# Addresses modulo 256 of the streamed tiles and of the low weight slices in a one-core decoder layer

## The chip, the cores and the metric

The kernel runs on one core of a Trainium2 chip. The metric is the device time of one execution in microseconds, here the median of three runs. Engines are named as in the profile: PE is TensorE's matmul, PEld TensorE's weight load, DVE VectorE, ACT ScalarE, POOL GpSimd, SP SyncE (which issues most DMAs).

## The reference

One layer of a hybrid decoder, on 256 prompt positions and 8 x 4 sample positions, which the kernel holds as 288 columns:

```python
x = x + 0.5 * swiglu(rms_norm(x, g1), w_gate1, w_up1, w_down1)      # D_MODEL 2048, D_FF 5632
z = rms_norm(x, gm) @ w_in                                           # u | q | k | v
y_ssm  = s5_mixer(u, ...)       # complex diagonal SSM, then GLU
y_attn = window_attention(q, k, v, ...)   # window 128, 16 query heads, 4 kv heads
x = x + concat(rms_norm(y_ssm), rms_norm(y_attn)) @ w_out
x = x + 0.5 * swiglu(rms_norm(x, g2), w_gate2, w_up2, w_down2)
```

All of it is in float32. The large matrix products (gate, up, down, w_in, w_out) make up nearly all of TensorE's work.

## The kernel before

**Three products for one.** Activations and weights are each split into a high part (rounded to the matmul's type fp32r) and a low part (the rest). One product of a 128 x 128 weight block with 128 x 288 activations is three matmuls, in `mm3` (L266 to L272): high weights by high activations (L270), high weights by low activations (L271), low weights by high activations (L272). Every matmul comes with a weight load of its own, so the high slice is loaded twice. While matmul j streams its 288 columns, TensorE loads the weights of matmul j+1; "streamed tile" is the moving operand, one of `xh[k]`, `xl[k]`, `hh`, `hl` (128 partitions x 288 values of 4 bytes, 1152 bytes in a partition), and "slice" is a weight block of 128 x 128 values (512 bytes in a partition).

So the loads go like this: while L270 streams the high tile of k, the high slice a is loaded again (for L271); while L271 streams the low tile of k, the low slice a is loaded (for L272); while L272 streams the high tile of k, the high slice a+1 is loaded (for the next L270).

**The stream of weights.** `Weights` walks a list of 680 pieces (up to 8 slices, 512 KB each; the down projection's are of 6 and 5 slices). `load` (L76) issues a DMA into a `raw` tile on SP's queue, `split` (L84) makes `wh` on ACT (L88) and `wl` on DVE (L89), and `next` (L102) hands one piece to the matmuls. Program order keeps the splits two pieces ahead of the matmuls and the loads five pieces ahead. A `raw` tile may be loaded again when its split is done; there are five. `wh` and `wl` have three buffers each.

**The stages.** `ffn(0)` runs first, to about 870 us; then `mix` (w_in, SSM and attention work, w_out), to about 1185 us; then `ffn(1)`. In `ffn`, gate and up (`gu`, streaming xh and xl, 16 values of k) fill a ring of h tiles, `hh` and `hl` of 13 buffers each, and after every 11 of them `down(c)` streams those 11 tiles for each of 16 output tiles: 33 matmuls to an output tile. w_out streams 8 tiles of pools with 8 buffers each.

**Addresses.** A partition's byte address of each tile follows from the order and sizes of the allocations. 1152 is 4 x 256 + 128, so tiles that follow one another alternate between two classes modulo 256 that are 128 apart. As the program is laid out:
- `xh[0]` and `xl[0]` both start at 128 modulo 256, since 16 tiles are a whole number of 256. So the order of streaming in gate, up and w_in is 128, 128, 128, then 0, 0, 0, and so on by k: three streamed tiles of one class, then three of the other. w_out's tiles (8 buffers each) go in the same way.
- `hh` and `hl` of a ring of 13 are in opposite classes, since 13 tiles are an odd number of 128. So the down projections stream a high, a low and a high tile of alternate classes, and the next k goes on alternating, except where the ring wraps and where one output tile ends and the next begins (tile 11 and tile 1 are of one class). The two classes are 64 and 192 in ffn(0), 32 and 160 in ffn(1), and all four in w_out.
- `wh` and `wl` buffers are 4096 bytes and start at 160 modulo 256, and slices are 512 bytes apart: every slice that is loaded starts at 160.

So in ffn(1)'s down projections a load is either in the very class of the tile that is streamed beside it (160 and 160) or in the opposite one (160 and 32), in turn. In the other stages the two are 32, 96, 160 or 224 apart.

## Time and profile before

| | |
|---|---|
| median of three runs | 2029.94 us (2029.13 to 2031.17) |
| the profiled execution | 2029.67 us |
| its span, first to last instruction | 2027.9 us |
| PE busy | 2006.7 us (99%) |
| matmuls of L270, L271 and L272 | 14400 (9408 stream xh or xl, 4992 stream hh or hl) |
| mean granted TensorE clock | 0.998 |

Busy times of PE count overlapping matmuls once. Since a matmul is recorded from its first column to its last result, about 295 ns, and the next one starts about 132 ns later, the pace of TensorE is read from the starts: in a stretch without other work, the time between two starts divided by the number of matmuls between them. The count is in the views too: a window's count is the steps in it and the two or three matmuls that reach into it from ahead or start at its end.

### The profile page before, as it was taken

To read this page: it belongs to the slowest core of one execution; us is meant where nothing else is said; L and a number is where in the kernel's file an instruction comes from. 1 tells how busy PE (TensorE), PEld (TensorE's weight loads), DVE (VectorE), ACT (ScalarE), POOL (GpSimd) and SP (SyncE) were. 2 spreads that over 40 slices of the span, in tenths; PEclk is the share of its full clock that TensorE was granted. 3 is DMA by queue.
4 is the path that set the end of the run, shared out by engine and by line. 5 is a ranking of instruction groups with operands and counts; after the bars stand their busy time and mean duration, and the time that the engine had idled before them with its cause. 6 is when DMAs were issued, how large, how long until landed. Compare 5 with 4: busy or idle time off the path is not lost. (4 is left out here: it accounts for less than half of the span.)

```text
span 2027.9 us, 37632 instructions
## 1 busy us (share of the span) xinstructions
PE 2006.7 (99%) x15248; PEld 1994.0 (98%) x15248; DVE 1211.4 (60%) x1873; ACT 850.6 (42%) x1334; POOL 296.1 (15%) x451
## 2 busy tenths in 40 slices
PE   8999999999999999999999999999999999999999
PEld 8999999999999999999989999999999999999999
DVE  5577666666656645676687874445445544454444
ACT  5433443444344434533466443333333333333332
POOL 3100011001110000212268630000000000000000
PEclk9999999999999999999999999999999999999999
DMA  6655656564556554678733445555555655565554
GB/s 225 201 163 151 211 162 197 170 209 166 196 169 196 180 198 140 215 231 269 237 118 131 152 161 166 166 149 181 167 166 151 186 162 166 149 180 170 167 158 149
DMA packets 122622, 359.04 MB, mean 177 GB/s; under 512 B 22448, under 2 KB 30256, under 8 KB 121264
## 3 DMA queue, kind: packets, MB, share of 16 engines
q1 hardware_dynamic: 114672, 340.81, 53.3%
q10 hardware_dynamic: 7776, 15.83, 2.3%
q8 instruction: 119, 1.95, 0.4%
q14 instruction: 55, 0.45, 0.1%
HBM read 338.40 MB, written 20.22 MB: 177 GB/s over the span
## 5 line engine op out<-in xcount | busy, mean ns | idle before, releaser
L89 DVE TENSOR_TENSOR wl<-raw,wh 128x1024 fp32r<-128x1024 f32 (+2 forms) x680 | 759.6, 1118 | 539.4 <-ACT wh L88 536.4
L270 PE MATMUL main<-xh,wh 128*128 128x288 f32 x3136 | 935.7, 298 | 6.2 <-ACT xh L178 6.2
L272 PE MATMUL main<-xh,wl 128*128 128x288 f32 x3136 | 932.7, 297 | 0.3 <-DVE wl L89 0.3
L271 PE MATMUL main<-xl,wh 128*128 128x288 f32 x3136 | 918.2, 293 | 1.3 <-DVE xl L179 1.3
L88 ACT CAST wh<-raw 128x1024 fp32r<-128x1024 f32 (+2 forms) x680 | 642.9, 946 | 625.2 <-PE main L271 414.8
L271 PEld LDWEIGHTS main<-xl,wh 128*128 128x128 f32 x3136 | 600.9, 192 | 2.4 <-DVE xl L179 2.1
L270 PEld LDWEIGHTS main<-xh,wh 128*128 128x128 f32 x3136 | 592.2, 189 | 7.3 <-ACT xh L178 6.2
L272 PEld LDWEIGHTS main<-xh,wl 128*128 128x128 f32 x3136 | 590.4, 188 | 0.6 <-DVE wl L89 0.6
L270 PE MATMUL main<-hh,wh 128*128 128x288 f32 x1664 | 494.4, 297 | 0.0
L271 PE MATMUL main<-hl,wh 128*128 128x288 f32 x1664 | 492.2, 296 | 0.3 <-DVE hl L667 0.3
L272 PE MATMUL main<-hh,wl 128*128 128x288 f32 x1664 | 491.4, 295 | 0.0
L271 PEld LDWEIGHTS main<-hl,wh 128*128 128x128 f32 x1664 | 313.6, 188 | 0.7 <-DVE hl L667 0.6
L270 PEld LDWEIGHTS main<-hh,wh 128*128 128x128 f32 x1664 | 313.6, 188 | 0.4
L272 PEld LDWEIGHTS main<-hh,wl 128*128 128x128 f32 x1664 | 313.7, 189 | 0.0
L296 POOL TENSOR_TENSOR s<-s,R 128x288 f32<-128x288 f32 x88 | 71.5, 812 | 1252.0 <-ACT s L295 1252.0
L295 ACT ACTIVATE s<-t 128x288 f32<-128x288 f32 x88 | 39.1, 445 | 237.9 <-DVE t L294 237.9
L303 ACT CAST hh<-h 128x288 fp32r<-128x288 f32 x88 | 38.1, 433 | 240.0 <-DVE h L302 240.0
L323 DVE SCALAR_TENSOR_TENSOR x<-main,x 128x288 f32<-128x288 f32 x128 | 58.3, 456 | 50.0 <-PE main L272 48.2
L302 DVE TENSOR_TENSOR h<-main,s 128x288 f32<-128x288 f32 x88 | 40.2, 457 | 77.4 <-PE main L272 76.9
L294 DVE TENSOR_TENSOR t<-main,R 128x288 f32<-128x288 f32 x88 | 40.2, 457 | 64.1 <-PE main L272 63.4
L304 DVE TENSOR_TENSOR hl<-h,hh 128x288 fp32r<-128x288 f32 x88 | 40.3, 458 | 43.9 <-ACT hh L303 43.9
L188 POOL TENSOR_TENSOR acc<-acc,sq 128x288 f32<-128x288 f32 x45 | 48.8, 1085 | 56.7 <-ACT sq L184 55.3
(263 smaller groups left out, 879.3 us busy)
## 6 DMA issues: line engine op xcount, KB each, us to landing
raw<-in_w_gu SPq DMA_DIRECT2D x352, 512.0 KB, 3.6
raw<-in_w_dn SPq DMA_DIRECT2D x128, 384.0 KB, 3.1
raw<-in_w_dn SPq DMA_DIRECT2D x128, 320.0 KB, 3.0
raw<-in_w_in SPq DMA_DIRECT2D x40, 512.0 KB, 4.2
raw<-in_w_out SPq DMA_DIRECT2D x32, 512.0 KB, 3.4
mats<-stage ACTq DMA_DIRECT2D x8, 1536.0 KB, 7.0
mb<-mats SPq DMA_DIRECT2D x8, 768.0 KB, 6.7
ma<-mats SPq DMA_DIRECT2D x8, 512.0 KB, 4.3
```

The costliest lines, as they stand in the source:

```text
L88: self.nc.scalar.copy(wh[:, :n], t[:, :n])
L89: self.nc.vector.tensor_tensor(wl[:, :n], t[:, :n], wh[:, :n].bitcast(F32), op=ALU.subtract)
L188: eng.tensor_tensor(acc, acc, sq, op=ALU.add)
L270: pe.matmul(ps, wh[:, s], rh[k], start=first and a == 0, stop=False)
L271: pe.matmul(ps, wh[:, s], rl[k], start=False, stop=False)
L272: pe.matmul(ps, wl[:, s], rh[k], start=False, stop=last and a == n - 1)
L294: dve.tensor_tensor(t1, pg[:, :N], R, op=ALU.mult)
L295: act.activation(s1, t1, AF.Silu)
L296: pool_e.tensor_tensor(s2, s1, R, op=ALU.mult)
L302: dve.tensor_tensor(h, pu[:, :N], s2, op=ALU.mult)
L304: dve.tensor_tensor(hl, h, hh.bitcast(F32), op=ALU.subtract)
L323: dve.scalar_tensor_tensor(x[d], ps[:, :N], 0.5, x[d], op0=ALU.mult, op1=ALU.add)
```

## The change

- A tile of 128 bytes (`gap_x`) is allocated between `xh` and `xl`, and one of 128 bytes between `hh` and `hl` of the rings and of the w_out pools (`gap_r`, `gap_y`). The rings have 14 buffers in place of 13. So the high and the low tile of a k are in opposite classes, and the streamed tiles alternate in every stage, still except from one output tile of a down projection to the next (11 tiles).
- `wl`'s slices are 640 bytes apart (`WLS` is 160 values), so that they alternate between two classes as well: slice a starts at 128 x a modulo 256. `wl` tiles are 5376 bytes in place of 4096. For chunks of the down projection whose first tile falls on an odd place of the ring, the slices start 128 bytes later (`shifted`). DVE's subtraction writes through a three-dimensional pattern, 8 x 128 with a step of 160.
- `gap_w`, `gap_p` and `gap_l` bring the pools behind them to the class that this needs: with `gap_x` and `gap_w`, the constants end at a multiple of 256, and `wh` and `wl` start at 0 modulo 256.
- `raw` has four buffers in place of five, which makes room.

No instruction is added or taken away, and none is moved in any queue. `wh`'s slices stay 512 bytes apart, so all of them start at 0 modulo 256, while the tiles streamed beside them go 128, 0, 128 for one k (high, low, high) and 0, 128, 0 for the next. Counted over six matmuls (two values of k), the loads beside the streamed tiles are: opposite class, same, opposite; same, same, same.

```diff
+WLS = P + 32
+RING = 14
...
-        t = self.pool.tile([P, HALF], F32, name="raw", bufs=5)
+        t = self.pool.tile([P, HALF], F32, name="raw", bufs=4)
...
-        wl = self.pool.tile([P, HALF], F32R, name="wl", bufs=3)
+        wl = self.pool.tile([P, 8 * WLS + 64], F32R, name="wl", bufs=3)
+        o = 32 if self.ns in self.shifted else 0
+        m = n // P
+        wl = wl[:, o:o + m * WLS].rearrange("p (a c) -> p a c", c=WLS)[:, :, :P]
         self.nc.scalar.copy(wh[:, :n], t[:, :n])
-        self.nc.vector.tensor_tensor(wl[:, :n], t[:, :n], wh[:, :n].bitcast(F32), op=ALU.subtract)
+        self.nc.vector.tensor_tensor(wl, t[:, :n].rearrange("p (a c) -> p a c", c=P),
+                                     wh[:, :n].bitcast(F32).rearrange("p (a c) -> p a c", c=P), op=ALU.subtract)
...
+                if j * CH % RING % 2:
+                    shifted.update(range(len(pieces), len(pieces) + 2 * KT))
...
     xh = [cp.tile([P, N], F32R, name="xh%d" % k) for k in range(KT)]
+    cp.tile([P, 32], F32, name="gap_x")
     xl = [cp.tile([P, N], F32R, name="xl%d" % k) for k in range(KT)]
...
     R = cp.tile([P, N], F32, name="R")
+    cp.tile([P, 56], F32, name="gap_w")
...
-            pe.matmul(ps, wl[:, s], rh[k], start=False, stop=last and a == n - 1)
+            pe.matmul(ps, wl[:, a], rh[k], start=False, stop=last and a == n - 1)
...
             hh = hp.tile([P, N], F32R, name="hh")
+            if f == 0:
+                hp.tile([P, 32], F32, name="gap_r", bufs=1)
             hl = hp.tile([P, N], F32R, name="hl")
...
-    with tc.tile_pool(name="ring1", bufs=13, reuse_waits="tile") as hp:
+    with tc.tile_pool(name="ring1", bufs=RING, reuse_waits="tile") as hp:
```

## Rows read from the trace of the kernel before

**Rows 1.** The page's first part (busy time, share of the span and instructions of each engine) and the granted TensorE clock in 40 slices of the span.

```profile
PE 2006.7 (99%) x15248; PEld 1994.0 (98%) x15248; DVE 1211.4 (60%) x1873; ACT 850.6 (42%) x1334; POOL 296.1 (15%) x451
...
PEclk9999999999999999999999999999999999999999
```

**Rows 2.** The groups by line and operation: the first matmul of the three, for the stages that stream x and those that stream h (out<-in, shapes, count, busy us, mean ns of one, idle us before them).

```profile
L270 PE MATMUL main<-xh,wh 128*128 128x288 f32 x3136 | 935.7, 298 | 6.2 <-ACT xh L178 6.2
...
L270 PE MATMUL main<-hh,wh 128*128 128x288 f32 x1664 | 494.4, 297 | 0.0
```

**Rows 3.** Busy times by window (start and end in us, length, then each engine's busy us and count, granted clock, DMA share and GB/s): a stretch that streams x, one of ffn(0)'s down projection, one of w_out, and two of ffn(1)'s down projection.

```profile
1211.25:1230.29 19.04, 19.04 (x147) 19.04 (x146) 9.63 (x11) 7.30 (x9) 0.81 (x1) 1.00 0.59 188
172.45:185.63 13.18, 13.18 (x101) 13.18 (x100) 11.91 (x23) 4.69 (x6) 0.04 (x1) 1.00 0.59 176
1152.75:1178.35 25.60, 25.60 (x194) 25.60 (x193) 24.23 (x26) 14.78 (x24) 22.23 (x18) 1.00 0.53 179
1338.97:1342.48 3.51, 3.51 (x30) 3.51 (x29) 2.24 (x3) 1.86 (x3) 0.00 (x0) 1.00 0.17 37
...
1355.61:1368.74 13.13, 13.13 (x101) 13.13 (x100) 6.72 (x9) 4.70 (x6) 0.00 (x0) 1.00 0.57 166
```

**Rows 4.** The timeline of PE (start us, duration us, line, operation, count) at the two ends of the stretch that streams x: 144 matmuls, six pieces of 24, lie between the two starts.

```profile
1211.25 0.29 PE L270 MATMUL main<-xh,wh 128*128 128x288 f32 x1
...
1230.29 0.29 PE L270 MATMUL main<-xh,wh 128*128 128x288 f32 x1
```

**Rows 5.** The same at the two ends of three output tiles (99 matmuls) of ffn(0)'s down projection.

```profile
172.45 0.29 PE L270 MATMUL main<-hh,wh 128*128 128x288 f32 x1
...
185.63 0.29 PE L270 MATMUL main<-hh,wh 128*128 128x288 f32 x1
```

**Rows 6.** The same at the two ends of eight pieces (192 matmuls) of w_out.

```profile
1152.75 0.30 PE L270 MATMUL main<-hh,wh 128*128 128x288 f32 x1
...
1178.35 0.30 PE L270 MATMUL main<-hh,wh 128*128 128x288 f32 x1
```

**Rows 7.** The timeline of PE in the first output tiles of ffn(1)'s down projection: 27 matmuls lie between the first two starts; from the third on, the first two of every four steps' starts are shown, with two left out.

```profile
1338.97 0.29 PE L270 MATMUL main<-hh,wh 128*128 128x288 f32 x1
...
1342.48 0.29 PE L270 MATMUL main<-hh,wh 128*128 128x288 f32 x1
...
1343.92 0.30 PE L272 MATMUL main<-hh,wl 128*128 128x288 f32 x1
1344.06 0.29 PE L270 MATMUL main<-hh,wh 128*128 128x288 f32 x1
...
1344.45 0.30 PE L270 MATMUL main<-hh,wh 128*128 128x288 f32 x1
1344.60 0.29 PE L271 MATMUL main<-hl,wh 128*128 128x288 f32 x1
...
1344.99 0.30 PE L271 MATMUL main<-hl,wh 128*128 128x288 f32 x1
1345.13 0.29 PE L272 MATMUL main<-hh,wl 128*128 128x288 f32 x1
...
1345.52 0.30 PE L272 MATMUL main<-hh,wl 128*128 128x288 f32 x1
1345.66 0.29 PE L270 MATMUL main<-hh,wh 128*128 128x288 f32 x1
...
1346.05 0.30 PE L270 MATMUL main<-hh,wh 128*128 128x288 f32 x1
```

**Rows 8.** One line of the code, L270, from 1339.3 to 1342.2 us: its matmuls and its weight loads (count, duration in ns as min/median/max, first and last start).

```profile
L270 PEld LDWEIGHTS main<-hh,wh x8: 187/188/188, 1339.2 to 1342.0; 128*128 128x128 f32 x8
L270 PE MATMUL main<-hh,wh x8: 291/292/293, 1339.4 to 1342.1; 128*128 128x288 f32 x8
```

**Rows 9.** The same line from 1344.0 to 1346.9 us.

```profile
L270 PEld LDWEIGHTS main<-hh,wh x8: 187/188/192, 1343.9 to 1346.7; 128*128 128x128 f32 x8
L270 PE MATMUL main<-hh,wh x8: 292/294/303, 1344.1 to 1346.9; 128*128 128x288 f32 x8
```

**Rows 10.** Busy times by window, columns as in rows 3: one piece of a gate or up projection in ffn(1), with its 24 matmuls.

```profile
1200.93:1204.11 3.18, 3.18 (x27) 3.18 (x25) 1.73 (x3) 1.38 (x2) 0.81 (x1) 1.00 0.00 0
```

**Rows 11.** The groups by line with shapes kept apart: DVE's subtraction of a whole piece.

```profile
L89 DVE TENSOR_TENSOR wl<-raw,wh 128x1024 fp32r<-128x1024 f32 x424 | 530.9, 1253 | 360.1 <-ACT wh L88 357.8 <-DMA raw<-in_w_gu 1.5 <-DMA ud<-t 0.5
```

**Rows 12.** SP's timeline: the issues of one piece's load, in ffn(0)'s last down projection, and of the next piece's.

```profile
813.99 0.34 SPq L80 DMA_DIRECT2D raw<-in_w_dn  x1
...
816.27 0.33 SPq L80 DMA_DIRECT2D raw<-in_w_dn  x1
```

**Rows 13.** The time from issue to landing of the load issued at 813.99 us (min/median/max of that one).

```profile
DMA to landing us min/median/max: 8.7/8.7/8.7
```

**Rows 14.** The timelines of ACT, DVE and PE at the copy, the subtraction and the first matmul of that same piece.

```profile
823.20 0.84 ACT L88 CAST wh<-raw 128x768 fp32r<-128x768 f32 x1 [0.54 <-PE main L271]
...
824.07 0.96 DVE L89 TENSOR_TENSOR wl<-raw,wh 128x768 fp32r<-128x768 f32 x1 [0.33 <-ACT wh L88]
...
827.48 0.30 PE L270 MATMUL main<-hh,wh 128*128 128x288 f32 x1
```

More of the change, by code (lines that the diff above doesn't have):

```diff
@@ L54, in __init__ @@
         self.raw, self.hl = {}, {}
+        self.shifted = set()
         self.nl = self.ns = 0
@@ L130, in tile_hymba_step @@
     pieces = []
+    shifted = set()
     def ffn_units(l):
@@ L165, in tile_hymba_step @@
     W = Weights(nc, wp, pieces)
+    W.shifted = shifted
     x = [cp.tile([P, N], F32, name="x%d" % k) for k in range(KT)]
     xh = [cp.tile([P, N], F32R, name="xh%d" % k) for k in range(KT)]
+    cp.tile([P, 32], F32, name="gap_x")
     xl = [cp.tile([P, N], F32R, name="xl%d" % k) for k in range(KT)]
@@ L360, in precompute @@
         rep = [small("rep%d" % i, (P, 4, 2, 16)) for i in range(2)]
+        small("gap_p", (P, 24))
         def vexp(src, em1=None, ex=None):
@@ L596, in shift_cache @@
         sp.dma_start(io["old_" + n], src.rearrange("b (r c) -> b r c", c=1024))
-    with tc.tile_pool(name="pre", bufs=1) as qp, tc.tile_pool(name="ring0", bufs=13) as hp:
+    with tc.tile_pool(name="pre", bufs=1) as qp, tc.tile_pool(name="ring0", bufs=RING) as hp:
         W.spread(24, precompute(qp))
@@ L658, in y_split @@
         hh = pool.tile([P, N], F32R, name="hh", bufs=8)
+        if first:
+            pool.tile([P, 32], F32, name="gap_y", bufs=1)
         hl = pool.tile([P, N], F32R, name="hl", bufs=8)
@@ L794, in ssm_done @@
         late["y"] = es.enter_context(tc.tile_pool(name="late_y", bufs=1, reuse_waits="tile"))
+        late["y"].tile([P, 24], F32, name="gap_l")
     hold = e["Hold"](W.i + 2)
```

## Prediction

> **What bounds the kernel now.** I read the page's busy times first. PE is busy 99% of the span, the other engines 60% and less, and the granted clock stands at full speed (2.4 GHz) in every slice of the page [rows 1]. So there is next to no waiting to save, and the time is a number of matmuls times their pace. The groups by line say how many: 3136 x 3 = 9408 matmuls that stream x (gate, up and w_in), and 1664 x 3 = 4992 that stream h [rows 2]; of the latter, by the code, 4 x 16 x 33 = 2112 are in each feed-forward's down projections and 768 in w_out. The idle time that this page shows before the costliest of these groups is 6.2 us.
>
> The pace is read from the timeline's starts, at the two ends of stretches without other matmuls; the windows confirm the counts (147 for 144 steps, and so on) [rows 3]. Where x is streamed: (1230.29 - 1211.25) / 144 = 132.2 ns [rows 4]. In ffn(0)'s down projection: (185.63 - 172.45) / 99 = 133.1 ns [rows 5]. In w_out: (1178.35 - 1152.75) / 192 = 133.3 ns [rows 6]. In ffn(1)'s down projection: (1368.74 - 1355.61) / 99 = 132.6 ns [rows 3]. These matmuls have one shape and type, at one clock. What differs between the stages is where the tiles lie. The differences are of 1 ns, but 1 ns on 14400 matmuls is 14.4 us, or 0.7% of the time.
>
> **How fast it can go.** ffn(1)'s down projection begins with a stretch that is faster than any of these: 27 matmuls in 1342.48 - 1338.97 = 3.51 us, 130.0 ns each [rows 7]. In it every matmul of L270 takes 291 to 293 ns and every load 187 or 188 [rows 8]. I call this the clean pace. From 1343.92 us on, in the same stage with the same two classes, every fourth step is long: 16 steps take 1346.05 - 1343.92 = 2.13 us, 133.1 ns each; the twelve between the long ones take 4 x 0.39 = 1.56 us, 130 ns each, which leaves 0.57 / 4 = 142 ns for a long one [rows 7]. There the longest matmul is of 303 ns and the longest load of 192 [rows 9]. So a matmul and the weight load beside it now and then lengthen each other, by 12 ns, and in a repeating pattern. By the program's addresses all the long steps shown are streams of the opposite class to the slice loaded beside them (32 against 160). None of them is a stream of the same class.
>
> Two other causes fall out. The DMA engines moved little in the clean stretch (share 0.17) [rows 3], but a piece that streams x with no DMA at all takes (1204.11 - 1200.93) / 24 = 132.5 ns a matmul, no less than the same stage with DMA at 0.59 [rows 3, 10]. And the clock is 1.00 in both.
>
> **The change, part by part.** *Classes of the streams and slices.* Every stage gets what ffn(1)'s down projections have now (alternating tiles, slices in the same or the opposite class), but with two opposite loads in six where that stage has three. How to price it: equal-class steps cost 130 ns; opposite ones alternate between 130 and 142 in the pattern of four, 136 on average. That stage as a whole is at 132.6, so it is in the pattern for (132.6 - 130.0) / (133.1 - 130.0) = 85% of its steps (rounded as such estimates deserve) and clean for the rest. With two opposite of six, the pattern would give (4 x 130 + 2 x 136) / 6 = 132.0 ns, and 0.85 x 132.0 + 0.15 x 130.0 = 131.7 ns. That is my pace for all stages. The sum: x, (132.2 - 131.7) x 9408 = 4.7 us; ffn(0)'s down, 1.4 x 2112 = 3.0; w_out, 1.6 x 768 = 1.2; ffn(1)'s down, 0.9 x 2112 = 1.9; in all 10.8 us less. No trace shows four loads in six of the streamed class, so the bounds are wide: clean throughout (130.0) below, the full pattern (133.1, in x too) above. I stay with the estimate between them since it is made from the stage whose classes are nearest.
>
> *The junctions.* In x's stages tiles alternate from one piece to the next as well, 16 being even. In down projections one junction in 33 stays in one class; the ring's wraps go. I count nothing for these, as 132.6 holds them.
>
> *The subtraction with steps of 640 bytes.* DVE writes the same 1024 values in eight rows; now it takes 1253 ns for a whole piece [rows 11]. The trace has no such pattern, so nothing to a half more (0.6 us) is my bound, and something less than nothing is not excluded; I take nothing. Its cover: for the piece below, DVE ends at 824.07 + 0.96 = 825.03 us and PE wants the slices at 827.48 [rows 14], 2.4 us later.
>
> *Four raw buffers.* A load waits for the split of the piece four ahead of it rather than five, so it is issued one split later, some 2.3 us in a down projection (813.99 to 816.27) [rows 12]. What is behind it on SP's queue (loads of SSM tables, caches and the final stores) moves back as much at most. The tightest load that I found is issued at 813.99 us and takes 8.7 us to land, being issued next to a cache's copy [rows 13]; ACT reads it at 823.20 [rows 14]. 2.3 us later it lands at 825.0, the split (0.84 us on ACT, then DVE to 825.03 when begun at 823.20) ends near 826.8, and PE wants it at 827.48. So 0.7 us of cover remain, and this costs nothing; if that cover went, a stall of 1 or 2 us at two places.
>
> *The 14th buffer and the gaps* add no instruction and no wait. A ring with one buffer more can only free a tile sooner.
>
> The sum against the profiled execution: 2029.67 - 10.8 = 2018.9 us. Its median neighbour is 2029.94, 0.01% off, so I don't correct for it; what lies around the span (1.8 us) stays.
>
> **The rivals.** *Clean nearly everywhere.* If fewer opposite loads, never two in a row in time with the pattern of four, mean that the pattern can't hold itself, the clean pace comes: 2.2 x 9408 + 3.1 x 2112 + 3.3 x 768 + 2.6 x 2112 = 20.7 + 6.5 + 2.5 + 5.5 = 35.2 us less, 1994.5 us. For it: with loads opposite, same, opposite, then three times the same, long steps four apart would fall on loads of the same class, where rows 7 show none. Against it: in its own stage the clean stretch is short, and the pattern came back after it.
>
> *Slower: the pattern of four in x's stages.* They run at 132.2 now, with slices that start 32 or 160 bytes above the streamed tile modulo 256, never 0 or 128. Moved there, they could fall in the pattern of four at 133.1 for good: 0.9 x 9408 = 8.5 us more, ffn(1)'s down 0.5 x 2112 = 1.1 more, w_out 0.2 less, ffn(0)'s as now: 2039 us. It is slower from the point where more than (132.2 - 130.0) / (133.1 - 130.0) = 71% of x's steps are in that pattern; ffn(1)'s down projection has 85%. For it: x's stages are the faster ones today and make up two thirds of the matmuls. Against it: one opposite load in three is taken away.
>
> *No difference.* If the 12 ns come from something that goes with the time and not with the classes (the order of the three matmuls, the h tiles), the paces stay and the time is 2029.7 us. For it: all paces of whole stages lie within 1.1 ns, though their classes differ, and one may think that most of what lies above the clean pace is there wherever the tiles are.
>
> The Trainium skill has a rule that speaks against this change: its page TensorE: Matmul & The Clock Gate, section Step-by-step: what each phase is for, says that TensorE has two independent read ports into SBUF and that loading the next weights takes no read bandwidth from the running matmul. By that rule the classes don't matter and this is the rival of no difference, at 2029.7 us. The trace doesn't bear it out in full: one line's loads take 187 to 192 ns and its matmuls 292 to 303, in the same stage and shape [rows 9], against 188 and 293 at most just before [rows 8]. The same page, section Back-to-back issue gap, has a gap of N / 2.4 + 2.5 ns for isolated matmuls, 122.5 ns as an estimate for 288 columns; by it 14400 matmuls could save some 140 us, but no stretch read here goes under 130.0.
>
> **How the numbers follow.** My forecast, a pace of 131.7 ns, 0.38; clean nearly everywhere 0.25; no difference 0.17; the pattern in x's stages 0.20. The predicted time is the forecast's, 2018.9 us. The range takes in the clean end and stops short of the whole of the slower one: 1992 to 2038 us. A measurement of this kernel can tell about 0.2%, 4 us, from no change. Faster by more: the clean case and nine tenths of the forecast, 0.59. Within it: no difference and a little of the forecast, 0.20. Slower by more: 0.21.
>
> **What would show it.** In the profile of the changed kernel, the pace between two starts where x is streamed: 131.7 by the forecast, 130 by the clean rival, 132.2 by no difference, 133 by the slower one. Durations of one line: 291 to 293 only, if clean; some of 302, with loads of 192, where the pattern holds. PE's idle time from DVE's `wl` or from ACT's `wh` should stay at nothing, and around 827 us above all, else the raw buffers were priced wrong. What makes the prediction wrong most easily is the dynamics: the paces come from a pattern that repeats, and a new order of classes may settle in one that no stage shows today, under 130 or above 133.

## The result, and the profile after

The changed kernel takes 2034.46 us in the median of 16 runs (2031.72 to 2039.72), the kernel before 2030.65 us in 16 runs beside it (2027.68 to 2033.48): 1.0019 times as long, with a 95% interval of 1.0011 to 1.0027. That is 3.8 us more, where the prediction had 10.8 us less. The profiled execution took 2034.44 us, with a span of 2032.7 us.

The page's first lines say the same as those of before [rows 1]: PE is busy nearly throughout, and the tenths of the granted clock show nothing.

```profile
PE 2008.1 (99%) x15248; PEld 1995.4 (98%) x15248; DVE 1211.9 (60%) x1873; ACT 851.4 (42%) x1334; POOL 295.8 (15%) x451
...
PEclk9999999999999999999999999999999999999999
```

So the time has to be taken apart, as before, into paces and stops. First the paces, from the timeline of PE (start us, duration us, line, operation, count). L283, L284 and L285 are now what L270, L271 and L272 were. Two starts with 147 matmuls between them, where x is streamed in ffn(1), and two with 192 between them in w_out:

```profile
1211.33 0.29 PE L283 MATMUL main<-xh,wh 128*128 128x288 f32 x1
...
1230.60 0.29 PE L283 MATMUL main<-xh,wh 128*128 128x288 f32 x1
...
1155.34 0.29 PE L283 MATMUL main<-hh,wh 128*128 128x288 f32 x1
...
1180.94 0.29 PE L283 MATMUL main<-hh,wh 128*128 128x288 f32 x1
```

(1230.60 - 1211.33) / 147 = 131.1 ns, where [rows 4] gave 132.2; and (1180.94 - 1155.34) / 192 = 133.3 ns, as in [rows 6]. One stretch is therefore faster, the other as it was. But a stretch doesn't speak for its stage. The table has the mean step from one start to the next over every step of a stage (steps over 160 ns left out, which are stops or halved clock), and what the difference makes over the stage's matmuls:

| stage | matmuls | before, ns | after, ns | difference, us |
|---|---|---|---|---|
| ffn(0), x | 4224 | 132.24 | 132.45 | +0.9 |
| ffn(0), down | 2112 | 133.13 | 132.24 | -1.9 |
| w_in | 960 | 132.27 | 132.48 | +0.2 |
| w_out | 768 | 133.26 | 132.87 | -0.3 |
| ffn(1), x | 4224 | 132.23 | 132.75 | +2.2 |
| ffn(1), down | 2112 | 132.57 | 132.39 | -0.4 |

The paces come to +0.7 us in this execution. The rest of the 4.8 us by which the span grew comes from one stage: from the first matmul of w_in to the first of w_out it took 1064.0 - 867.0 = 197.0 us before and takes 1068.6 - 865.4 = 203.2 us now, 6.2 us more, while what lies ahead of it and behind it took 1.4 us less in all. The waits of PE (line waited, releaser and its line; us in total, times, longest) show the stops of that stage, after:

```profile
PE main L734 <- DMA rot<-mats: 2.9, 1, 2.9
PE main L795 <- DMA gl<-in_w_glu: 2.5, 2, 1.3
PE main L217 <- POOL acc L689: 2.5, 1, 2.5
...
PE main L734 <- DMA U<-ud: 1.5, 1, 1.5
```

and before (L716, L777 and L204 are the same lines as L734, L795 and L217):

```profile
PE main L716 <- DMA U<-ud: 2.6, 2, 1.5
...
PE main L777 <- DMA gl<-in_w_glu: 1.4, 1, 1.4
...
PE main L204 <- POOL acc L671: 1.0, 1, 1.0
```

PE now waits 2.9 us for the small table `rot` and 1.1 us more for `gl`, 1.1 less for `U`, and 1.5 more at L217. That last one doesn't belong to the change as such: the same program has 1.0 us there in its second profile (after_look2, below), and alt_raw5 has 2.5 with five buffers. After the stop on `rot` the granted clock falls. The windows (start:end, length, PE's busy us and count, granted clock, DMA share, GB/s), after and then before:

```profile
890.00:897.00 7.00, 4.07 (x32) 0.98 0.80 250
897.00:900.50 3.50, 3.50 (x18) 0.55 1.00 356
```

```profile
890.00:897.00 7.00, 5.95 (x49) 1.00 0.61 190
897.00:900.50 3.50, 3.50 (x28) 1.00 0.97 347
```

PE was busy for 4.07 of 7 us, and in the next 3.5 us it ran at 0.55, near the lower of its two levels (1.2 GHz against 2.4), with 18 matmuls where it had 28 before. In full, the trace has the half clock for 3.4 us from 896.8 us, and again from 917.2 us, where before has it once in this part of the span, from 914.7 us. A step takes 240 ns in it (three of them from 898.76 to 899.48 us) and not some 132, so such a stretch costs about 1.5 us.

### The profile page after: what moved, and what is told of

Same layout as the page of the kernel before. It is cut to its first block, busy times and chain, and to the rows that moved or that the text cites. A ratio compares the mean times of both kernels' runs of the same rounds, so it can differ in the third digit from the quotient of the medians.

```text
span 2032.7 us, 37629 instructions
## 1 busy us (share of the span) xinstructions
PE 2008.1 (99%) x15248; PEld 1995.4 (98%) x15248; DVE 1211.9 (60%) x1873; ACT 851.4 (42%) x1334; POOL 295.8 (15%) x451
## 5 line engine op out<-in xcount | busy, mean ns | idle before, releaser
L283 PE MATMUL main<-xh,wh 128*128 128x288 f32 x3136 | 931.5, 297 | 6.2 <-ACT xh L191 6.2
L284 PE MATMUL main<-xl,wh 128*128 128x288 f32 x3136 | 929.9, 297 | 1.3 <-DVE xl L192 1.3
L285 PE MATMUL main<-xh,wl 128*128 128x288 f32 x3136 | 926.9, 296 | 0.0
L283 PEld LDWEIGHTS main<-xh,wh 128*128 128x128 f32 x3136 | 592.1, 189 | 7.4 <-ACT xh L191 6.2
L284 PEld LDWEIGHTS main<-xl,wh 128*128 128x128 f32 x3136 | 592.5, 189 | 2.4 <-DVE xl L192 2.1
L285 PEld LDWEIGHTS main<-xh,wl 128*128 128x128 f32 x3136 | 593.4, 189 | 0.2 <-DVE wl L95 0.2
L284 PE MATMUL main<-hl,wh 128*128 128x288 f32 x1664 | 491.6, 295 | 0.3 <-DVE hl L685 0.3
L283 PE MATMUL main<-hh,wh 128*128 128x288 f32 x1664 | 491.8, 296 | 0.0
L285 PE MATMUL main<-hh,wl 128*128 128x288 f32 x1664 | 490.6, 295 | 0.0
L284 PEld LDWEIGHTS main<-hl,wh 128*128 128x128 f32 x1664 | 313.0, 188 | 0.7 <-DVE hl L685 0.5
L283 PEld LDWEIGHTS main<-hh,wh 128*128 128x128 f32 x1664 | 313.0, 188 | 0.4
L285 PEld LDWEIGHTS main<-hh,wl 128*128 128x128 f32 x1664 | 313.3, 188 | 0.0
```

The source lines that it names most:

```text
L283: pe.matmul(ps, wh[:, s], rh[k], start=first and a == 0, stop=False)
L284: pe.matmul(ps, wh[:, s], rl[k], start=False, stop=False)
L285: pe.matmul(ps, wl[:, a], rh[k], start=False, stop=last and a == n - 1)
```

## The experiments

There are three groups: the four buffers, the pace by itself, and the layer with other classes. Each timed kernel ran on one chip together with the kernel before, and its ratio is to those runs.

### Four raw buffers

**before_raw4** is the kernel before with one number changed.

```diff
-        t = self.pool.tile([P, HALF], F32, name="raw", bufs=5)
+        t = self.pool.tile([P, HALF], F32, name="raw", bufs=4)
```

> The kernel before with four raw buffers in place of five, all else as it was; addresses modulo 256 are unchanged. If the loss sits in the loads that now stand on SP's queue ahead of the mix stage's table loads (the buffer theory), it is 4 to 7 us slower than before, with PE waits on DMA loads of rot, U or gl of 2 us and more in the w_in stage, and paces as before (132.2 where x is streamed). If four buffers cost nothing, as the prediction had it, it is within 1 us of before.

2034.71 us (11 runs, before 2030.41): 1.0020 (1.0011 to 1.0028). This one number by itself costs as much as the whole change does. Its paces are those of before in every stage, to 0.03 ns.

**alt_raw5** is the other half: the high and low tiles in opposite classes (`gap_x`, `gap_r`, `gap_y`, 14 ring buffers), but `wl` with slices 512 bytes apart, which needs no room, and five raw buffers.

```diff
-            pe.matmul(ps, wl[:, s], rh[k], start=False, stop=last and a == n - 1)
+            pe.matmul(ps, wl[:, a], rh[k], start=False, stop=last and a == n - 1)
...
+    cp.tile([P, 32], F32, name="gap_x")
...
+    with tc.tile_pool(name="ring1", bufs=RING, reuse_waits="tile") as hp:
```

> The changed kernel with five raw buffers and with low slices 512 bytes apart, so only the streamed tiles' classes are changed: they alternate in all stages, and all slices are of one class, 0 modulo 256. By the buffer theory the mix stage is as before and the time follows the paces alone. If equal classes are the cheap ones, half of the loads are opposite: 132.6 ns where x is streamed, and the time is 2030 to 2034 us. If alternating tiles by themselves bring the clean pace, 130 to 131 ns and 2005 to 2015 us. If any order gives about the same, 132.2 to 133 ns and 2029 to 2038 us.

2031.50 us (11 runs, before 2030.41): 1.0011 (0.9999 to 1.0023). Paces of its profile sum to 1.6 us more than before. It is not told apart from no change. One thing went against the expectation: its profile, of an execution of 2035.24 us, took 203.0 us from w_in to w_out, as long as the changed kernel's, with 4.1 us of waiting for `U`. So five buffers don't rule such a passage out in a single execution, and what four of them cost is read from the medians of before_raw4 above and raw4_la4 below, not from one profile.

**after_swap** and **after_la4** keep the whole change and take the load of the piece out of the way of what stands behind it on SP's queue: the one by letting the work that is spread over the pieces, small loads among it, be issued first, the other by issuing each load one piece later.

```diff
 after_swap, in next():
-        self.prime(i + self.la + 1)
         while self.fill.get(i):
...
         self.fill.pop(i, None)
+        self.prime(i + self.la + 1)
 after_la4, in Weights:
-    def __init__(self, nc, pool, pieces, load_ahead=5, split_ahead=2):
+    def __init__(self, nc, pool, pieces, load_ahead=4, split_ahead=2):
```

> The changed kernel with one order swapped: in each step the other work (table loads on SP among it) is issued ahead of the next piece's load, so that it does not stand behind a load that waits for a raw buffer. By the buffer theory the 5 to 6 us that the w_in stage lost come back: 2028 to 2031 us, level with before. If the loss comes from the addresses, it stays at 2034.

2032.61 us (12 runs, before 2030.41): 1.0013 (1.0002 to 1.0025). This lies between what the theory expected and the rival's 2034, and its interval overlaps that of the changed kernel, so it decides nothing.

**raw4_la4** puts the second of these edits on before_raw4, where the classes can't blur it.

> The kernel before with four raw buffers, and each load issued one piece later (four pieces ahead, not five), so that the load at the head of SP's queue waits for the same split as in the kernel before and what stands behind it in the queue waits no longer than there. Theory (the 4 us of four buffers come from the small loads of rot, U and gl that stand in SP's queue behind a load whose buffer is not yet free): they come back, 2029 to 2032 us, 0.9995 to 1.001 of the kernel before, and in w_in the waits for rot, U and gl are 4 us in all or less. Rival (the pieces themselves land too late with one buffer less): no better than four buffers alone, 2034 us or more, 1.002 and up, with PE waiting for wl or wh.

> The changed kernel with each load issued one piece later (four pieces ahead, not five) and its four buffers and classes as they are. Theory: the queue's 4 us come back and only the classes are left, whose paces sum to 0.7 us more than before: 2029 to 2033 us, 0.9995 to 1.001. Rival (late pieces): 2034 us or more, 1.002 and up.

raw4_la4: 2030.17 us (12 runs, before 2029.49): 1.0001 (0.9993 to 1.0010). All of the loss is gone, with four buffers. The pieces that now come later stop nothing; PE waits for `wl` 0.3 us in all, as before (before_raw4 had 1.1). This is the queue, then, and not the pieces. The waits of PE for small loads in before_raw4, then in raw4_la4:

```profile
PE main L716 <- DMA U<-ud: 5.9, 3, 2.6
PE main L777 <- DMA gl<-in_w_glu: 2.0, 2, 1.3
```

```profile
PE main L716 <- DMA U<-ud: 2.4, 3, 1.2
...
PE main L777 <- DMA gl<-in_w_glu: 0.5, 2, 0.3
```

How it happens is to be seen on SP's queue at the start of w_in (start us, duration us, line, what is loaded, count). In the changed kernel:

```profile
885.90 5.45 SPq L83 DMA_DIRECT2D raw<-in_w_in  x2
891.40 1.85 SPq L709 DMA_DIRECT2D U<-ud  x4
893.30 0.43 SPq L717 DMA_DIRECT2D rot<-mats  x1
```

In the kernel before, then in raw4_la4:

```profile
886.04 1.83 SPq L80 DMA_DIRECT2D raw<-in_w_in  x2
890.36 3.13 SPq L691 DMA_DIRECT2D U<-ud  x4
893.60 0.38 SPq L699 DMA_DIRECT2D rot<-mats  x1
```

```profile
887.47 1.83 SPq L80 DMA_DIRECT2D raw<-in_w_in  x2
891.62 2.80 SPq L691 DMA_DIRECT2D U<-ud  x4
894.46 0.43 SPq L699 DMA_DIRECT2D rot<-mats  x1
```

The two piece loads occupy the queue for 5.45 us instead of 1.83, since the second one waits for a split, and `U` and `rot` stand behind them. Counted from the first matmul of w_in (865.4, 867.0 and 868.5 us), `U` is issued at 26.0, 23.4 and 23.1 us, and `rot` at 27.9, 26.6 and 26.0 us. Between 860 and 1030 us the profile of before_raw4 had the half clock for 10.2 us, and both profiles of the changed kernel for 6.8; those of raw4_la4, after_swap and all three of after_la4 had none there, and before had 3.4 us.

after_la4: 2033.80 us (11 runs, before 2029.49): 1.0016 (1.0006 to 1.0025). Here the time came back in small part, if at all. So something else in the change costs time too. It keeps all else that the change has, the classes as well as the strided subtraction and the 14th buffer, and which of these it is was not tested; the classes are the likely part, as the paces were higher than before's in all five profiles of the changed kernel and of after_la4 (last table of the experiments). The half clock isn't it: the mean granted clock of these 11 executions is 0.998, like that of the 23 of before.

### The pace by itself

**mb1_paces**, **mb2_orders** and **mb3_starts** compute nothing of the layer: they leave all of it out, and write zeros. Each is a row of stretches of matmuls from one buffer of activations and one of weights, with next to nothing beside them (the DMA share is 0.00 from 540 to 1130 us of mb1_paces), and what differs is the byte offsets (`w` is the slice, `o` the streamed tile) and, in a few stretches, the number of columns or of weights:

```python
ps = pm.tile([P, 512], F32, name="ps")
for i in range(288):
    o, w = [0, 1152][i % 2] // 4, [1152, 0][i % 2] // 4
    pe.matmul(ps[:128, :288], BW[:, w:w + 128], BX[:, o:o + 288], start=i == 0, stop=i == 287)
```

> This kernel computes nothing of the layer and writes zeros; it only measures paces. TensorE runs 28 stretches of 288 matmuls, one after the other, each stretch with its own order of byte addresses for the streamed tile and for the weight slice: ten stretches with one tile and one slice at a distance of 0 to 384 bytes modulo 512, four with two tiles of alternate classes and one slice, four in which the slices follow the streamed tile at a fixed distance of 0, 64, 128 or 192, two with the orders of the kernel before and after where x is streamed, and eight with other numbers of columns or of weights. If equal classes are the cheap ones (the forecast's theory), one tile with the slice at distance 0 is at 130 ns and at 128 it is at 133 to 136; slices that follow at 0 are at 130, those that follow at 128 at 133 or above. If instead the pace is set by a repeating pattern that any order of classes falls into (the rival), all 128 x 288 stretches lie between 130 and 134 ns with no order by distance, and the orders of before and after are within 0.7 ns of each other. If the load beside the stream costs nothing, the stretch with 64 weight columns has the pace of that with 128.

The timeline of PE shows a whole stretch in a row (start, length, line, operation, count), so the pace is the difference of two rows' starts by 288. L151, L156, L161, L166: tiles alternating between the two classes, and the slice loaded beside each 0, 64, 128 and 192 bytes above its class modulo 256. L171 and L176: the addresses where x is streamed, of before and of the changed kernel. L181 and L196: one tile and one slice, with 256 and 512 columns. L206: one tile and one slice, with 64 weight columns in place of 128.

```profile
543.77 37.61 PE L151 MATMUL ps<-bx,bw 128*128 128x288 f32 x288
581.22 38.25 PE L156 MATMUL ps<-bx,bw 128*128 128x288 f32 x288
619.31 38.88 PE L161 MATMUL ps<-bx,bw 128*128 128x288 f32 x288
658.02 38.56 PE L166 MATMUL ps<-bx,bw 128*128 128x288 f32 x288
696.42 38.24 PE L171 MATMUL ps<-bx,bw 128*128 128x288 f32 x288
734.50 38.55 PE L176 MATMUL ps<-bx,bw 128*128 128x288 f32 x288
772.89 34.71 PE L181 MATMUL ps<-bx,bw 128*128 128x256 f32 x288
807.43 42.41 PE L186 MATMUL ps<-bx,bw 128*128 128x320 f32 x288
...
899.60 65.48 PE L196 MATMUL ps<-bx,bw 128*128 128x512 f32 x288
964.92 32.30 PE L201 MATMUL ps<-bx,bw 128*128 128x192 f32 x288
997.06 37.60 PE L206 MATMUL ps<-bx,bw 128*64 128x288 f32 x288
1034.50 37.92 PE L211 MATMUL ps<-bx,bw 128*32 128x288 f32 x288
```

The four distances give 130.0, 132.3, 134.4 and 133.3 ns. So where the slice lies against the tile does matter, with no DMA and no other engine beside it, by up to 4.4 ns. One tile and one slice gave 131.7 ns at 0 and 256 and 133.3 at 128 and 384, as a period of 256 would have it; but in this form 160 gave 131.7 as well, and 32, 64, 96 and 224 gave 133.3, so the opposite class is not the one dear place. By the columns: 119.9, 146.7 and 226.8 ns for 256, 320 and 512, which is the columns at 2.4 GHz plus 13.3 ns. L206, with half the weight columns at the addresses that gave 131.7 ns, ran at 130.0; no stretch of 288 columns was faster. The stretch with the addresses of before's x stage (L171) gave 132.2 ns, that of the changed kernel's (L176) 133.3: alone in this kernel, the change is slower.

> Computes nothing of the layer and writes zeros; 28 more stretches of matmuls that differ in addresses and order. Ten have two tiles of alternate classes and slices that follow the streamed tile at 0 to 240 bytes: by the theory that every load must be in the class of the tile streamed beside it, 130.0 ns at 0 and more at every other distance, most at 128. Then orders of the three products: by pairs of k (high by high for both, high by low for both, low by high for both), with high and low tile of a k in one class, the next k in the other, and slices in alternate classes, every load is in the streamed tile's class: 130.0 ns; the same with the slices in the other class 134.4; the same with all slices in one class 132 to 133.4. The orders of the kernels before and after again, run after another stretch: 132.2, and 131 or 133.3 if that order has two patterns as the trace of after suggests. If the rival (any order falls into some pattern of 132 to 133.4) is right, the pairs are there too.

The same offsets as in L151 now gave 132.7 ns, not the 130.0 that was expected. Distances of 16, 32 and 48 bytes gave 133.3, 134.4 and 136.7 ns, and 240 gave 130.0. The order of products by pairs of k (below), every slice in the class of the streamed tile, gave 132.7 (130.0 was expected), and every slice in the opposite one 134.4. The orders of the kernels before and after gave 132.2 and 133.3 ns again.

> Microbenchmark that computes nothing of the layer. Nine distances between the class of the streamed tile and that of the weight slice that is loaded meanwhile (0, 4, 8, 248, 244, 240, 236, 232, 224 bytes, modulo 256), every load at the same distance, and each distance started six times after one matmul of another length (40, 104, 168, 200, 250, 310 columns), so that the stretch begins at six different phases; 120 matmuls of 280 columns each. Theory A (distance alone sets the pace; the two paces seen at distance 0, 130.0 and 132.67 ns, are two phases in which a stretch can settle): the six starts at distance 0 fall on both 130.0 and 132.67, and at distance 240 all six give 130.0 (that distance gave 130.01 in the one stretch seen). Rival B (the two paces come from something outside, not from the start): the six starts of one distance agree with each other to 0.1 ns.

Each distance was begun six times, after one matmul of another length; the matmuls have 288 columns, not 280. Rows of the starts at distance 0 (L83), 120 matmuls each:

```profile
39.27 16.12 PE L83 MATMUL ps<-bx,bw 128*128 128x288 f32 x120
...
55.32 15.78 PE L83 MATMUL ps<-bx,bw 128*128 128x288 f32 x120
...
71.06 16.08 PE L83 MATMUL ps<-bx,bw 128*128 128x288 f32 x120
```

From their starts, steady paces of 132.66, 130.03 and 132.67 ns: the same addresses settle in one of two patterns, and which one differs from start to start. (No start was run twice, so whether the start decides it or chance does is not shown.) The distance of 248 bytes did so too (130.00 and 132.2), and 240 (131.67, one at 133.37, and 130.0 in mb2_orders); the other six distances gave one pace to 0.1 ns each, from 131.67 (8 bytes) to 133.3 (244 and 224). So theory A's two paces came at 0, and its 130.0 for all starts at 240 did not; for six distances the starts agree, as rival B has it.

### Other classes in the layer

**pairs** keeps five raw buffers and puts every load, of `wh` too, in the class of the tile streamed beside it. For that the products are ordered by pairs of k, `wh` and `wl` share a tile, and even and odd slices lie in two halves of it.

```diff
-            pe.matmul(ps, wh[:, s], rh[k], start=first and a == 0, stop=False)
-            pe.matmul(ps, wh[:, s], rl[k], start=False, stop=False)
-            pe.matmul(ps, wl[:, s], rh[k], start=False, stop=last and a == n - 1)
+            for a, k in pair:
+                pe.matmul(ps, wh[a], rh[k], start=first and a == 0, stop=False)
+            for a, k in pair:
+                pe.matmul(ps, wh[a], rl[k], start=False, stop=False)
+            for a, k in pair:
+                pe.matmul(ps, wl[a], rh[k], start=False, stop=last and not todo and a == pair[-1][0])
```

**pairs_opp** is pairs with `gap_w` 128 bytes longer, so that in the x stages every load is in the opposite class. **pairs_order** is the order of the products alone, at the addresses of before.

> The whole layer with the kernel before's five raw buffers, the products issued by pairs of k as in the last measurement, and both weights' slices in alternate classes (even and odd slices in two halves of a tile that are 4224 bytes apart), so that every load but those at the ends of the down projections' output tiles is in the class of the tile streamed beside it. If equal classes give the clean pace once all loads have them: 130 ns where x is streamed and 130.5 in the down projections, 28 to 34 us less than before, 1996 to 2003 us. If the pace is a pattern that comes anyway: 132 to 133.3 ns, 2028 to 2040 us.

> The same with the weights' buffers 128 bytes further on, so that where x is streamed every load is in the opposite class; the down projections and w_out are as in the kernel with pairs. Instructions are the same. If the classes decide: 134.4 ns where x is streamed, 4.4 x 9408 ns or 41 us more than with pairs. If they don't: level with pairs.

> The kernel before with the order of products by pairs of k alone, at the addresses of before, so streamed tiles alternate where x is streamed and slices start 32 or 160 above them. If alternating tiles alone were what helps: 130 to 131 ns where x is streamed, some 15 to 20 us less than before. If the classes of the loads are needed: 132.2 to 133.4 ns, from level with before to 11 us more.

Ratios to 9 runs of the kernel before at 2029.88 us:

| kernel | median us | ratio to before | ffn(1) x, ns | sum of paces, us |
|---|---|---|---|---|
| pairs | 2017.60 (5 runs) | 0.9932 (0.9917 to 0.9947) | 130.67 | 1890.3 |
| pairs_opp | 2042.62 (4 runs) | 1.0069 (1.0051 to 1.0086) | 134.43 | 1918.3 |
| pairs_order | 2038.59 (4 runs) | 1.0042 (1.0028 to 1.0056) | 133.33 | 1916.6 |

(The sum is 1907.6 us for the kernel before, 1908.3 for the changed one.) From the timeline, where x is streamed in ffn(1): pairs, then pairs_opp.

```profile
1199.89 0.42 PE L287 MATMUL main<-xh,w 128*128 128x288 f32 x2
...
1229.53 0.42 PE L287 MATMUL main<-xh,w 128*128 128x288 f32 x2
```

```profile
1200.25 0.43 PE L287 MATMUL main<-xh,w 128*128 128x288 f32 x2
...
1230.10 0.30 PE L287 MATMUL main<-xh,w 128*128 128x288 f32 x1
```

29.64 us for 228 matmuls is 130.0 ns, 29.85 for 222 is 134.5. Nothing but the place of the slices against the tiles differs, so in the layer too the classes matter. pairs itself fell short of its expectation: its paces sum to 17.3 us less than before, not 28 to 34, above all as ffn(0)'s x stage stayed at 132.1 ns, and the time fell by 12.3 us; where the other 5 us went is not shown. The order of products is no help in itself; it costs.

> The kernel of pairs with the weight slices 16 bytes lower than the class of the streamed tile, in all stages. If a distance of 240 bytes settles at 130.0 ns wherever a stretch starts, the x stages lose the stretches at 132.67 ns: 9,400 matmuls by up to 2.1 ns less (the x stage of pairs in ffn(0) is at 132.1 on average), most of it in ffn(0), w_in and w_out: some 10 us less than pairs, 2005 to 2012 us. If phase decides and not distance, it is within 4 us of pairs (2017.6 us). If a distance other than 0 costs (16 bytes the other way gave 133.33 ns), 133.3 ns and 2035 us.

> The kernel of pairs once more, beside pairs_240 on one chip: 2017.6 us again (2011 to 2019), 0.993 of the kernel before. If its x stages settle in other phases from one execution to the next, single executions spread over more than the 7 us seen.

pairs_240: 2021.11 us (6 runs, before 2031.57): 0.9952 (0.9934 to 0.9970), paces of 131.7 ns in ffn(1)'s x stage. Some 10 us less than pairs was expected; it is 7 us more than pairs_again, beside it. pairs_again: 2014.06 us (6 runs, the same before): 0.9913 (0.9893 to 0.9933). The same program ran its first x stage at 132.10 ns on average in the one profile and at 131.49 in the other. The timeline at the same place, pairs (198 matmuls), then pairs_again (204):

```profile
46.56 0.43 PE L287 MATMUL main<-xh,w 128*128 128x288 f32 x2
...
72.83 0.43 PE L287 MATMUL main<-xh,w 128*128 128x288 f32 x2
```

```profile
46.57 0.42 PE L287 MATMUL main<-xh,w 128*128 128x288 f32 x2
...
73.08 0.42 PE L287 MATMUL main<-xh,w 128*128 128x288 f32 x2
```

132.7 and 130.0 ns: which pattern a stretch settles in is not fixed by the program. These two profiles are from different chips, so the chip could be the cause.

**after_look2, after_la4_look2, after_la4_look3** ask whether the pattern is drawn anew in each execution of the changed kernel; the three are from one chip.

> The changed kernel once more, for a second profiled execution of the same program. Theory (the same addresses settle in one of two patterns, and which one is drawn anew in each execution): the mean pace where x is streamed differs by over 0.2 ns from the 132.45 and 132.75 ns of the first profile in at least one of the two feed-forwards, with the time moving by the sum of that. Rival (the pattern is fixed by the program): 132.45 and 132.75 within 0.05 ns.

> The changed kernel with loads four pieces ahead once more, for a second profiled execution. The first one took 2028.9 us, with 132.45 and 133.30 ns where x is streamed and one stretch of halved clock inside the span, while the median of 11 executions was 2033.8. Theory: a slower execution shows other paces, or one stretch of halved clock more (1.7 us each). Rival: the same paces and stretches at another time, so that the difference lies elsewhere.

> A third profiled execution of the same kernel, with the same two expectations.

| profile | time, us | ffn(0) x, ns | ffn(1) x, ns | sum of paces against before, us |
|---|---|---|---|---|
| the changed kernel | 2034.44 | 132.45 | 132.75 | +0.7 |
| after_look2 | 2038.99 | 132.93 | 133.33 | +5.0 |
| after_la4 | 2028.90 | 132.45 | 133.30 | +2.2 |
| after_la4_look2 | 2030.77 | 132.39 | 132.75 | +0.2 |
| after_la4_look3 | 2032.12 | 132.45 | 133.31 | +2.2 |

It is: after_la4_look2 and after_la4_look3 are one program on one chip, and differ by 0.56 ns in ffn(1). after_look2 differs from the first profile by 0.5 and 0.6 ns, and took 4.6 us longer, with 4.3 us of it in the paces. The first stretch shown in the section on the result, in after_la4_look3 (147 matmuls from the first row to the last):

```profile
1211.13 0.30 PE L283 MATMUL main<-xh,wh 128*128 128x288 f32 x1
1211.27 0.30 PE L284 MATMUL main<-xl,wh 128*128 128x288 f32 x1
1211.41 0.29 PE L285 MATMUL main<-xh,wl 128*128 128x288 f32 x1
...
1230.74 0.29 PE L283 MATMUL main<-xh,wh 128*128 128x288 f32 x1
```

133.4 ns, where the first profile had 131.1. The x stages of before, of before_raw4 and of raw4_la4, which have one set of addresses, were at 132.23 or 132.24 ns in both feed-forwards. The changed kernel draws between a pattern that is 1.1 ns faster than that and one that is 1.1 ns slower, and its sum was higher than before's in all five profiles, by 2.1 us on average. The times of the after_la4 profiles don't follow their paces: after_la4_look3 has the paces of the first and the same single stretch of half clock inside the span, and took 3.2 us longer, 1.9 of it between w_in and w_out, where it waited 3.7 us for `gl` in place of 0.8.

## Why the prediction was wrong

**The paces: 10.8 us less was forecast, 0.7 us more came in the profile, and up to 5.0 in another execution.** The step that failed is the pricing of single steps, "equal-class steps cost 130 ns; opposite ones alternate between 130 and 142". It was read from a stretch of [rows 7] in which every long step was an opposite one. In the changed kernel, all loads beside L284's streams (the low slices) are of the streamed class, and the mean step that begins with L284 is the longest of the three: 134.3 ns in ffn(1)'s x stage, against 131.6 for L283 and 132.3 for L285, which both have an opposite load in every second step. In the pattern of 133.3 ns, which repeats after 6 steps, the long step is in all five profiles one of L284's, 138 ns with a load of the streamed class (1211.27 to 1211.41 in the rows of after_la4_look3). In that of 131.1 ns, which repeats after 18, it is one of L285's, 140 ns with an opposite load. So the cost doesn't stay with the step that has the opposite load; it is the repeating pattern's. Counting opposite loads (two in six for three in six) therefore priced nothing. What held is that classes matter: all loads in the streamed class, 130.0 or 132.7 ns; all in the opposite one, 134.4. With only `wl` in the right class the pattern is 131.1 or 133.3, hardly another mean than the 132.2 and 133.3 of before. By parts: ffn(0)'s down projection gave 1.9 us of the forecast 3.0, w_out 0.3 of 1.2, ffn(1)'s down 0.4 of 1.9, and x lost 3.3 us (w_in's among it) where 4.7 were to be gained.

**The rivals.** The slower rival named the place, the x stages, and its pace (133.1) is about the slow one of the two patterns; it took the pattern of [rows 7] for it, which isn't the one that came, and held it for fixed. "Clean nearly everywhere" needs `wh` in class as well: pairs has 130.0 ns over long stretches. "No difference" is right to 0.2% in time, for another reason than it gave: two effects, none of them zero. That the time lies inside the stated range is luck as well: the range reached up there for the slower rival, and the buffers, which brought the time up by as much, were put at nothing.

On the Trainium skill's rule (TensorE: Matmul & The Clock Gate, section Step-by-step: what each phase is for), by which loading the next weights takes nothing from the running matmul, the measurement decides: with only the slices' place changed by 128 bytes, the stretches L151 and L161 of mb1_paces run at 130.0 and 134.4 ns.

**The buffers: "costs nothing" was forecast, and by themselves they cost 4 us** (before_raw4). The prediction had the mechanism in hand: a load is issued one split later, and what is behind it on SP's queue "moves back as much at most". It then worked out the cover for a piece (0.7 us left, and indeed this profile has no stop on `wl` or `wh`, at 827 us or elsewhere) and none for what stands behind. `U`, `rot` and `gl` have no cover: PE waited 2.6 us for `U` and 1.4 for `gl` before, a row of the waits that the prediction doesn't use. The price named for a lost cover, 1 or 2 us at two places, is about that of the stops; what it lacked is the clock after them, at half for 3.4 us or more.

**The subtraction** was rightly taken as free. The groups by line, with the forms apart, have the mean of [rows 11] to the nanosecond:

```profile
L95 DVE TENSOR_TENSOR wl<-raw,wh 128x1024 fp32r<-128x1024 f32 x424 | 530.9, 1253 | 364.5 <-ACT wh L94 363.5 <-DMA ma<-mats 0.5
```

**What stays open.** What makes the patterns is not shown, only that they depend on places modulo 256 and differ from start to start. A load is recorded for 187 or 188 ns [rows 8], longer than a step, so it reaches into the next stream too, and which of the two streams it meets badly is not shown either. The two costs hardly add: buffers alone 1.0020, the change without the queue's wait 1.0016, both together 1.0019 (1.0011 to 1.0027), where the sum would be 1.0036; but that sum is itself uncertain by some 0.0013, so this is at the edge of the noise. The five profiles' paces explain 2 us of what the rest of the change costs, and after_la4's median is 4.3 us above before; its three profiled executions (two of them on another chip) were all faster than that median, so the rest wasn't seen. And alt_raw5's profile has 10.2 us of half clock in w_in with five buffers, so these stretches don't come from the buffers alone.

## What to carry to other kernels

A difference in pace that comes from a repeating pattern can't be priced by its steps: measure the whole sequence by itself, with several starts, before moving a tile for it, and change the places of all slices that take part, as pairs did together with the order of products (0.993 and 0.991), or none. When a buffer is taken from a queue's first customer, look up the waits for everything that is issued behind it; if a load can only wait, issue it later (raw4_la4 gave the buffer up at no measurable cost).

## What was not expected of the hardware

- Steady streams of matmuls, each with a weight load, step at one of some paces between 130.0 and 136.7 ns for 288 columns at the full clock, by the slice's place against the streamed tile modulo 256 (mb1_paces, mb2_orders, mb3_starts). With slices that follow the tile, 48 bytes above is the worst seen (136.7), and 0, 240 and 248 have the best in some of their stretches.
- At 0 and 248 bytes there are two paces (130.0 and 132.7 or 132.2 ns), which differ from start to start and are then kept for at least 120 matmuls (mb3_starts).
- With one tile and one slice, 13.3 ns lie above the columns' own time at 2.4 GHz for 256, 320 and 512 columns (mb1_paces); the best seen is 10 ns (130.0 for 288, slices following the tile). Half the weight columns lowered the step at 288 columns (131.7 to 130.0 ns) and raised it at 512 (226.8 to 230.0).
- In the changed kernel a stop of PE of 2.9 us was followed within 2 us by the half clock for 3.4 us, which cost another 1.5 us or so. At the half clock a step took 240 ns, which is 288 columns at 1.2 GHz with nothing above.
